# Loading expert weights 2 MB at a time, 16 KB to a partition, with two more buffers, in a mixture-of-experts encoder layer

## The chip, the cores and the metric

The kernel runs on one core of one Trainium2 chip. The metric is the device time of one execution in microseconds, the median of the timed runs. Sizes are counted as in the profile's list of loads: 1 MB here is 1024 KB.

## What is computed

One layer of a bidirectional encoder over 512 tokens of width 1024, in float32: three token mixers in parallel, a cross-attention into 256 memory tokens, and a mixture of 16 experts in which every expert picks 64 tokens. The change touches the experts alone. Cut to them, the reference is:

```python
def ec_moe(h, router_w, w_gu, w_down):          # h: (1, 512, 1024)
    cap = 2 * n // 16                           # 64 tokens for each of 16 experts
    aff = jax.nn.softmax(logits, axis=-1)
    gates, idx = lax.top_k(jnp.swapaxes(aff, 1, 2), cap)
    xs = jax.vmap(lambda hb, ib: hb[ib])(h, idx)
    def expert(args):
        xe, wgu, wd = args                      # wgu: (1024, 4096), wd: (2048, 1024)
        gu = jnp.einsum('bcd,df->bcf', xe, wgu)
        ga, up = jnp.split(gu, 2, axis=-1)
        return jnp.einsum('bcf,fd->bcd', jax.nn.silu(ga) * up, wd)
    ys = lax.map(expert, (jnp.swapaxes(xs, 0, 1), w_gu, w_down))
```

An expert's weights are 16 MB of `expert_w_gu` and 8 MB of `expert_w_down`; all 16 experts together are 384 MB, each byte read once.

## The kernel before, in words

**Stages.** The mixers and the cross-attention come first (up to about 377 us in the profile), then the experts one after another, then a final norm and the store. A scheduler of the language places the instructions of each engine in one fixed order when the kernel is built; waits between engines are on semaphores.

**Buffers for expert weights.** `chunks` numbers the weights in pieces of 1 MB, 24 to an expert: pieces 0 to 15 are of `expert_w_gu` (piece j holds 128 of the 1024 input rows, `j // 2`, and one half of the 4096 columns, `j % 2`), pieces 16 to 23 of `expert_w_down`. A buffer of 2048 words on each of 128 partitions, a *slot*, holds one piece. Slots are cut from regions of SBUF (`rc`, `r1`, `rq`, `r2a`, `rd`, `ra`, `rb`, `f0`, `rp`, `fb`) as the earlier stages let go of them: `open_slots` makes one and has it filled at once by `issue`, which takes the next number of `order` and starts the load on SP's queue. There are 22 slots, of which four (two `acc` in `f0`, one in `rp`, one in `fb`) are filled once; when the last matmul on a piece in one of the other 18 has been written down, `done` calls `issue` again for that slot. So 22 MB are loaded before the first expert begins.

**A load of `expert_w_gu`** (L868) moves 128 rows of 2048 floats, 8 KB contiguous for each partition. **A load of `expert_w_down`** (L876) views the matrix as `(k p) d -> p k d`: partition p gets row p of two blocks of 128 rows, two runs of 4 KB. The last expert's `expert_w_down` is cut by columns (`LAST`, 512, 256 and 256 wide), with runs of 2 KB and 1 KB, so that the final norm can begin early.

**The matmuls.** For each half of the columns and each input block, L1251 multiplies the 64 gathered tokens with 512 columns of the piece at a time, into the two 64-partition halves `ab` of a PSUM bank. The columns for `ab` are four runs of 128 words with 128 words between them:

```python
wv = w.f[:, b * 1024:(b + 1) * 1024].rearrange("p (i ab c) -> p i ab c", ab=2, c=128)
T.matmul(pg[2 * half + b][64 * ab:64 * ab + 64], xs.f[:, k, el * 64:(el + 1) * 64],
         wv[:, :, ab], start=(k == 0), stop=(k == KT - 1))
```

After SiLU and product (L1263, L1264), L1267 turns eight 128-wide blocks so that the inner features lie on partitions, and L1282 multiplies them with `expert_w_down`, one piece for two of its 16 blocks of 128 inner features. The scatter of expert e - 1 (L1208, L1209, L1218) and, every other expert, the gather of the next two (L1180) are placed among these. L1316 is the last expert's product with `expert_w_down`.

In the profile each of these float32 matmuls stands as two PE instructions (eight for one piece of 1 MB).

Of the kernel before, what the change touches and what calls it, by code (L numbers as in the profile page):

```python
# [98 lines left out]
def build(nc, tc, A, out, ne=NE, dbg=None):  # L99
# [82 lines left out]
    idn = ident.f  # L182
# [652 lines left out]

    slots = []
    gu = A["expert_w_gu"][0]
    wd = A["expert_w_down"][0]
    chunks = [(e, j) for e in range(ne) for j in range(24)]

    where = {}
    once = {}
    order = list(range(15)) + list(range(16, 22)) + [15] + list(range(22, len(chunks)))
    order = iter(order)


    LAST = (512, 256, 256)

    def down_part(e, j):

        if e < ne - 1:
            return 2 * (j - 16), 2, 0, D
        j, c = j - 16, 0
        for w in LAST:
            n = w // 128
            if j < n:
                return 16 // n * j, 16 // n, c, w
            j, c = j - n, c + w

    def issue(s):  # L860
        i = next(order, None)
        if i is None:
            return
        where[i] = s
        e, j = chunks[i]
        if j < 16:
            src = gu[e, (j // 2) * 128:(j // 2 + 1) * 128, (j % 2) * 2048:(j % 2 + 1) * 2048]
            SP.dma_start(s.f, src)  # L868
        else:
            v = wd[e].rearrange("(k p) d -> p k d", p=128)  # L870
            k, nk, c, nc_ = down_part(e, j)
            d, v = s.f.rearrange("p (k d) -> p k d", k=nk), v[:, k:k + nk, c:c + nc_]

            h = nk // 2 if i in (22, len(chunks) - 1) else nk
            for a in range(0, nk, h):
                SP.dma_start(d[:, a:a + h], v[:, a:a + h])  # L876

    def open_slots(arena, n, use=None):
        for _ in range(n):
            s = Buf(arena, [SLOT])  # L880
            if use:
                once.setdefault(use, []).append(s)
            issue(s)

    ss2, rs2, tm2, sc2 = (sm.f[:, 16 + 4 * i:20 + 4 * i] for i in range(4))
# [423 lines left out]
    for i, w in enumerate(LAST):  # L1309
        py = (SC if i % 2 else MM)()[:, :w]  # L1310
        for _ in range(w // 128):
            k, nk, _, _ = down_part(ne - 1, next(parts))
            wv = chunk().f.rearrange("p (k d) -> p k d", k=nk)
            for j in range(nk):
                ab, blk = (k + j) % 2, (k + j) // 2
                T.matmul(py[64 * ab:64 * ab + 64], hT.f[:, blk, 64 * ab:64 * ab + 64], wv[:, j],  # L1316
                         start=(blk == 0), stop=(blk == 7))
        split(py, flat(yh.f)[:, c0:c0 + w], flat(yl.f)[:, c0:c0 + w])
# [88 lines left out]
```

## Time and profile before

| | before |
|---|---|
| median of 3 runs | 1320.96 us (1319.33 to 1323.13) |
| the profiled execution | 1321.95 us |
| its span on the core | 1320.2 us |
| PE busy | 1227.5 us (93%) |
| DVE, ACT, POOL busy | 448.4, 273.7, 115.8 us |
| moved by DMA | 434.87 MB (of 10^6 bytes) |

The span is the time from the core's first instruction to its last in one profiled execution; the execution's own time is 1.75 us longer. "Busy" is the union of an engine's instructions. In the views, DMA is the mean busy share of the core's 16 DMA engines, GB/s what they moved, and PEclk the granted clock of TensorE as a share of full speed.

### The profile page before, as it was taken

The numbers are of one execution on the slowest core, as the hardware profiler recorded it, in microseconds if no ns is written. First come the engines' busy times: TensorE is split into PE (matmuls) and PEld (weight loads), VectorE is DVE, ScalarE is ACT, GpSimd is POOL, SyncE is SP. The second block draws the span as 40 slices with busy tenths as digits, with TensorE's granted clock in tenths as the row PEclk, the third lists the DMA queues.
The fourth block names the chain that finished last, engine by engine and source line by source line (L and its number), as shares of the span: only waits on it lengthen the run. The fifth ranks groups of instructions, "written<-read, shape, count | busy, mean of one in ns | idle before, by whom it ended". The sixth has DMA issues, their size and how long they took to land.

```text
span 1320.2 us, 15788 instructions
## 1 busy us (share of the span) xinstructions
PE 1227.5 (93%) x6257; PEld 625.9 (47%) x6257; DVE 448.4 (34%) x1035; ACT 273.7 (21%) x579; POOL 115.8 (9%) x157
## 2 busy tenths in 40 slices
PE   9899898999989999999999899889989998998885
PEld 9887587788843343343343243224323322432223
DVE  5998758626730212212312122121202121221313
ACT  6565644315401001010010101000000101010013
POOL 5433143103000000000000000000000000000012
PEclk9999999999999999999999999999999999999998
DMA  8221040317879999999999999999999999999995
GB/s 290 81 65 49 20 161 33 128 35 308 322 273 367 418 416 419 417 417 415 419 414 421 414 421 414 419 416 417 418 415 420 413 421 414 421 414 419 417 409 207
DMA packets 97338, 434.87 MB, mean 329 GB/s; under 512 B 7536, under 2 KB 25584, under 8 KB 64496
## 3 DMA queue, kind: packets, MB, share of 16 engines
q1 hardware_dynamic: 97264, 433.87, 82.2%
q8 instruction: 49, 0.80, 0.2%
q14 instruction: 25, 0.20, 0.0%
HBM read 431.74 MB, written 2.10 MB: 329 GB/s over the span
## 4 chain that ended last, share of the span: by engine, by line
PE 60%; DMA 25%; DVE 8%; ACT 3%; issue 1%; SPq 0%; POOL 0%; DVEq 0%; ACTq 0%; POOLq 0%
PE mm L1251 19%; PE sc L1282 9%; PE oo L1251 6%; PE tr L1180 5%; DMA r_f<-in_expert_w_down 5%; DMA rq_f<-in_expert_w_gu 5%; DMA rq_f<-in_expert_w_down 3%; DMA ra_f<-in_expert_w_down 3%; DMA rb_f<-in_expert_w_gu 3%; DMA r2a_f<-in_expert_w_gu 3%; PE mm L125 3%; PE mm L127 3%; PE mm L126 3%; PE tr L1208 2%; PE tr L1209 2%; DMA r_f<-in_expert_w_gu 2%
## 5 line engine op out<-in xcount | busy, mean ns | idle before, releaser
L1218 DVE SCALAR_TENSOR_TENSOR f_f<-tr,f_f 128x512 f32<-128x512 f32 x112 | 79.9, 746 | 91.5 <-PE tr L1209 91.5
L1251 PE MATMUL mm<-rq_f,rg_f 128*64 128x512 f32 x388 | 97.3, 604 | 6.8 <-DMA rq_f<-in_expert_w_gu 6.8
L133 DVE TENSOR_TENSOR rp_r<-sc,rp_r 128x512 fp32r<-128x512 f32 (+1 forms) x31 | 21.1, 682 | 215.7 <-ACT rp_r L132 215.7
L1251 PE MATMUL mm<-r_f,rg_f 128*64 128x512 f32 x324 | 80.3, 602 | 5.8 <-DMA r_f<-in_expert_w_gu 5.4
L1180 PEld LDWEIGHTS tr<-f_f 128*128 128x128 f32 x512 | 61.7, 191 | 45.5 <-issue 23.5
L1301 POOL TENSOR_SCALAR f_f<-f_f 128x128 f32<-128x128 f32 x8 | 3.3, 434 | 907.5 <-PE tr L1196 880.4
L1264 DVE TENSOR_TENSOR fb_f<-mm,fb_f 128x512 f32<-128x512 f32 x16 | 11.1, 692 | 205.3 <-PE mm L1251 199.4
L1180 PE MATMUL tr<-f_f 128*128 128x128 f32 x512 | 70.8, 284 | 7.5 <-ACT rg_f L1187 4.7
L1263 ACT ACTIVATE fb_f<-mm 128x512 f32<-128x512 f32 x32 | 19.0, 597 | 279.0 <-PE mm L1251 279.0
L1187 ACT ACTIVATE rg_f<-tr,f_f 128x128 f32<-128x128 f32 x32 | 11.8, 368 | 271.7 <-PE tr L1180 181.6
L1282 PE MATMUL sc<-rq_f,fb_f 128*64 128x512 f32 x280 | 64.6, 599 | 3.6 <-DMA rq_f<-in_expert_w_down 3.6
L1185 DVE TENSOR_SCALAR rg_f<-tr,f_f 128x128 f32<-128x128 f32 x32 | 11.2, 351 | 157.6 <-PE oo L1251 78.7
L1251 PE MATMUL mm<-rb_f,rg_f 128*64 128x512 f32 x240 | 59.6, 603 | 4.1 <-DMA rb_f<-in_expert_w_gu 4.1
L1282 PE MATMUL sc<-r_f,fb_f 128*64 128x512 f32 x240 | 57.3, 600 | 4.3 <-DMA r_f<-in_expert_w_down 4.3
L1208 PE MATMUL tr<-rp_r 128*128 128x512 f32 (+1 forms) x132 | 58.2, 444 | 3.3 <-ACT rp_r L132 1.4
L132 ACT CAST rp_r<-sc 128x512 fp32r<-128x512 f32 (+1 forms) x31 | 17.9, 579 | 199.6 <-PE sc L1282 199.6
L1209 PE MATMUL tr<-rp_r 128*128 128x512 f32 (+1 forms) x132 | 53.2, 407 | 1.8 <-DVE rp_r L133 1.1
L1208 PEld LDWEIGHTS tr<-rp_r 128*128 128x128 f32 x132 | 24.5, 187 | 55.8 <-DVE f_f L1218 31.5
L1251 PEld LDWEIGHTS mm<-rq_f,rg_f 128*64 128x64 f32 x388 | 24.3, 136 | 55.7 <-issue 34.6
L1251 PE MATMUL mm<-r2a_f,rg_f 128*64 128x512 f32 x192 | 46.5, 603 | 3.3 <-DMA r2a_f<-in_expert_w_gu 3.3
L127 PE MATMUL mm<-r_r,rb_r 128*128 128x256 f32 (+2 forms) x160 | 47.4, 300 | 0.0
L1251 PE MATMUL oo<-rq_f,rg_f 128*64 128x512 f32 x172 | 45.1, 593 | 0.0
(451 smaller groups left out, 2207.8 us busy)
## 6 DMA issues: line engine op xcount, KB each, us to landing
rq_f<-in_expert_w_gu SPq DMA_DIRECT2D x70, 1024.0 KB, 19.8
r_f<-in_expert_w_gu SPq DMA_DIRECT2D x54, 1024.0 KB, 19.8
rb_f<-in_expert_w_gu SPq DMA_DIRECT2D x45, 1024.0 KB, 19.8
rq_f<-in_expert_w_down SPq DMA_DIRECT2D x35, 1024.0 KB, 19.9
r2a_f<-in_expert_w_gu SPq DMA_DIRECT2D x32, 1024.0 KB, 19.8
r_f<-in_expert_w_down SPq DMA_DIRECT2D x30, 1024.0 KB, 20.0
ra_f<-in_expert_w_gu SPq DMA_DIRECT2D x26, 1024.0 KB, 19.9
rb_f<-in_expert_w_down SPq DMA_DIRECT2D x18, 1024.0 KB, 18.8
```

The lines of the kernel that those rows point to most:

```text
L125: T.matmul(o, lh, rh, start=start, stop=False)
L126: T.matmul(o, lh, rl, start=False, stop=False)
L127: T.matmul(o, ll, rh, start=False, stop=stop)
L132: C.copy(h.bitcast(F32R), src)
L133: (le or V).tensor_tensor(l.bitcast(F32R), src, h, op=ALU.subtract)
L1180: i = T.matmul(o, x.f[:, t, kt * 128:(kt + 1) * 128], flat(g.f[:, t]), start=(t == 0), stop=(t == NT - 1))
L1208: T.matmul(pp[:, i * w:(i + 1) * w], GT.r[:, ts_], flat(yh.r)[:, cs], start=True, stop=False)
L1209: T.matmul(pp[:, i * w:(i + 1) * w], GT.r[:, ts_], flat(yl.r)[:, cs], start=False, stop=True)
L1218: V.scalar_tensor_tensor(ao, p, g, ao, op0=ALU.mult, op1=ALU.add)
L1251: T.matmul(pg[2 * half + b][64 * ab:64 * ab + 64], xs.f[:, k, el * 64:(el + 1) * 64], wv[:, :, ab], start=(k == 0), stop=(k == KT - 1))
L1263: C.activation(hsl.f[:, b], pg[b], AF.Silu)
L1282: T.matmul(py[c][64 * ab:64 * ab + 64], hT.f[:, blk, 64 * ab:64 * ab + 64], wv[:, ab, c * 512:(c + 1) * 512], start=(blk == 0), stop=(blk ...
```

## The change

Seven things change together.

1. Slots are 4096 words now (2 MB), except one each in `rc`, `rq`, `rd` and `rb` and the four that are filled once, which keep 2048 words.
2. When a 2 MB slot takes an even piece and the one after it, both come in one load: for `expert_w_gu` 128 rows of 4096 floats, 16 KB contiguous to a partition.
3. The inner features are interleaved over the partitions: `expert_w_down` is viewed as `(c p r) d`, so that partition p holds rows 4p to 4p + 3 of a block of 512 rows. A 2 MB load then has 16 KB contiguous to a partition, a 1 MB load 8 KB. To match, column c of a 1024-wide block of `expert_w_gu` goes to half `ab = c % 2` (every other word is read by a matmul), and the transposes at L1267 take every other column of `hsl`.
4. A slot is refilled when all pieces in it are used (`s.left`).
5. A new region `ex` of 4096 words, from space that the build had kept for descriptors of software-made DMAs (`dynamic_dma_scratch_size=512`), holds one more 2 MB slot. It is opened right after the weave of `att_0`, in the first stage.
6. The first expert's 24 pieces are all loaded ahead, in a new `order`.
7. The last expert's column slices have the same run lengths as before; its 256-wide pieces are loaded in two halves each.

```diff
-WORDS = {"rp": 3072, "rg": 1024, "ra": 4096, "rb": 6144, "rc": 2048, "rd": 2048, "r2a": 4096, "r1": 8448, "rq": 10240, "fb": 2048}
-WORDS["f0"] = 53000 - sum(WORDS.values())
+WORDS = {"rp": 3072, "rg": 1024, "ra": 4096, "rb": 6144, "rc": 2048, "rd": 2048, "r2a": 4096, "r1": 8448, "rq": 10240, "fb": 2048, "ex": 4096}
+WORDS["f0"] = 57096 - sum(WORDS.values())
...
+    order = [0, 1, 2, 3, 4, 6, 7, 8, 9, 10, 11, 5, 12, 13, 14, 16, 18, 19, 22, 20, 21, 17, 23, 15]
+    order += range(24, len(chunks))
...
+    def load_chunk(i, d):
+
+        e, j = chunks[i]
+        n = d.shape[-1] // SLOT
+        if j < 16:
+            src = gu[e, (j // 2) * 128:(j // 2 + 1) * 128, (j % 2) * 2048:(j % 2 + n) * 2048]
+            dma = SP.dma_start(d, src)
+            if i < 2:
+                tc.keep_in_program_order(dma)
+            return
+        k, nk, c, w = down_part(e, j)
+        nk *= n
+        if nk < 3:
+            r = 2 * (k % 2)
+            v = wd[e].rearrange("(c p r) d -> c p r d", p=128, r=4)[k // 2, :, r:r + 2 * nk, c:c + w]
+            SP.dma_start(d.rearrange("p (r d) -> p r d", d=w), v)
+        else:
+            v = wd[e].rearrange("(c p r) d -> p c r d", p=128, r=4)[:, k // 2:(k + nk) // 2, :, c:c + w]
+            d = d.rearrange("p (c r d) -> p c r d", r=4, d=w)
+            for a in range(nk // 2):
+                SP.dma_start(d[:, a], v[:, a])
+
+    def issue(s):
+        n = s.n // SLOT
+        ids, order[:n] = order[:n], []
+        for a, i in enumerate(ids):
+            where[i] = s, s.f[:, a * SLOT:(a + 1) * SLOT]
+        s.left = len(ids)
+        if n == 2 and ids and ids[0] % 2 == 0 and ids[1] == ids[0] + 1 and ids[0] < len(chunks) - 8:
+            load_chunk(ids[0], s.f)
+        else:
+            for i in ids:
+                load_chunk(i, where[i][1])
...
     run(fill)
+    open_slots(Arena(sp, "ex"), 1)
     for t in range(NT):
         turn(t, QT)
...
-    def done(s):
-        if id(s) not in kept:
+    def done(w):
+        s = w[0]
+        s.left -= 1
+        if not s.left and id(s) not in kept:
             issue(s)
...
-                    wv = w.f[:, b * 1024:(b + 1) * 1024].rearrange("p (i ab c) -> p i ab c", ab=2, c=128)
+                    wv = w[1][:, b * 1024:(b + 1) * 1024].rearrange("p (c ab) -> p ab c", ab=2)
...
-                T.transpose(p[:, i * 128:(i + 1) * 128], hsl.f[:, b, i * 128:(i + 1) * 128], idn)
+                T.transpose(p[:, i * 128:(i + 1) * 128], hsl.f[:, b, i // 2 * 256 + i % 2:(i // 2 + 1) * 256:2], idn)
...
-    nc = _bacc.Bacc("TRN2", target_bir_lowering=False, num_devices=1)
+    nc = _bacc.Bacc("TRN2", target_bir_lowering=False, num_devices=1, dynamic_dma_scratch_size=512)
```

What the built program issues differs most on SP, which starts the loads. Of the kernel before, the last 20 of one steady expert's 24 loads (names are the region that is written, `r1` without its number, and the tensor that is read; x4 is four loads in a row):

```order
L868 DMA rd_f<-in_expert_w_gu 128x2048
L868 DMA ra_f<-in_expert_w_gu 128x2048 x2
L868 DMA rb_f<-in_expert_w_gu 128x2048 x3
L868 DMA r_f<-in_expert_w_gu 128x2048 x2
L868 DMA rc_f<-in_expert_w_gu 128x2048
L868 DMA r_f<-in_expert_w_gu 128x2048 x2
L868 DMA rq_f<-in_expert_w_gu 128x2048
L876 DMA rq_f<-in_expert_w_down 128x2x1024 x4
L876 DMA r2a_f<-in_expert_w_down 128x2x1024 x2
L876 DMA rd_f<-in_expert_w_down 128x2x1024
L876 DMA ra_f<-in_expert_w_down 128x2x1024
```

The same stretch of SP in the changed program, one steady expert without its last load, an `rb` of 2 MB:

```order
L500 DMA ra_f<-in_expert_w_gu 128x4096
L500 DMA rb_f<-in_expert_w_gu 128x4096
L500 DMA ex_f<-in_expert_w_gu 128x4096
L500 DMA r_f<-in_expert_w_gu 128x4096
L500 DMA rc_f<-in_expert_w_gu 128x2048
L500 DMA rq_f<-in_expert_w_gu 128x2048
L500 DMA r_f<-in_expert_w_gu 128x4096
L500 DMA rq_f<-in_expert_w_gu 128x4096 x2
L509 DMA r2a_f<-in_expert_w_down 128x4096
L509 DMA rd_f<-in_expert_w_down 128x2048
L509 DMA rb_f<-in_expert_w_down 128x2048
L509 DMA ra_f<-in_expert_w_down 128x4096
```

Two loads in three are twice as large, the others stay at 1 MB, and the order of the pieces is the same. Counted over the whole program, behind the first 24 pieces come 96 loads of 2 MB and 48 of 1 MB of `expert_w_gu`, and 45 of 2 MB and 22 of 1 MB of `expert_w_down` before the last expert's slices.

In the first stage SP's rows around the new early load, in the changed program (L224 loads the mixers' weights, of which the first four shown are two sets and the next two the third set, `pl`; L807 loads the memory tokens):

```order
L224 DMA rq_f<-in_w_in 128x4x264 x3
L224 DMA rq_f<-in_w_in 128x4x256 x4
L500 DMA ex_f<-in_expert_w_gu 128x4096
L224 DMA rq_f<-in_w_in 128x4x256 x2
L224 DMA rq_f<-in_ca_wkv 128x4x256 x2
L807 DMA rq_f<-in_memT 128x4x256 x2
```

Before, the six loads of 128x4x256 stand there without a break; on the other engines the rows ahead of the first expert are unchanged.

## Rows read from the trace of the kernel before

**Rows 1.** From the profile's page: busy time of PE, and the span in 40 equal slices (33 us each) with the granted clock, the DMA engines' busy share in tenths, and GB/s.

```profile
PE 1227.5 (93%) x6257; PEld 625.9 (47%) x6257; DVE 448.4 (34%) x1035; ACT 273.7 (21%) x579; POOL 115.8 (9%) x157
...
PE   9899898999989999999999899889989998998885
...
PEclk9999999999999999999999999999999999999998
DMA  8221040317879999999999999999999999999995
GB/s 290 81 65 49 20 161 33 128 35 308 322 273 367 418 416 419 417 417 415 419 414 421 414 421 414 419 416 417 418 415 420 413 421 414 421 414 419 417 409 207
```

**Rows 2.** The chain of work that ended last, in order of time, over the last expert: start, length, what.

```profile
1221.04 20.37 DMA ra_f<-in_expert_w_down
...
1241.47 19.82 DMA r_f<-in_expert_w_gu
...
1261.36 19.83 DMA r2a_f<-in_expert_w_gu
...
1281.23 1.08 PE mm L1251 x4
```

**Rows 3.** PE's instructions in order of time while it multiplies the last expert's `expert_w_gu`: the first and the last of eight groups that begin with the landing of a load (in brackets the idle time before, and what ended it).

```profile
1263.82 1.94 PE L1251 MATMUL mm<-r_f,rg_f 128*64 128x512 f32 x8 [0.42 <-DMA r_f<-in_expert_w_gu]
1266.31 1.08 PE L1251 MATMUL mm<-rq_f,rg_f 128*64 128x512 f32 x4 [0.55 <-DMA rq_f<-in_expert_w_gu]
...
1281.23 1.08 PE L1251 MATMUL mm<-r2a_f,rg_f 128*64 128x512 f32 x4 [0.55 <-DMA r2a_f<-in_expert_w_gu]
```

**Rows 4.** The same for the `expert_w_down` of the expert before it: the five groups that begin with a landing.

```profile
1231.24 1.94 PE L1282 MATMUL sc<-rq_f,fb_f 128*64 128x512 f32 x8 [0.61 <-DMA rq_f<-in_expert_w_down]
1233.90 1.94 PE L1282 MATMUL sc<-r2a_f,fb_f 128*64 128x512 f32 x8 [0.71 <-DMA r2a_f<-in_expert_w_down]
...
1241.45 1.94 PE L1282 MATMUL sc<-ra_f,fb_f 128*64 128x512 f32 x8 [0.60 <-DMA ra_f<-in_expert_w_down]
```

**Rows 5.** DMA packets in two stretches: 1242 to 1281 us, mostly `expert_w_gu`, and 1221 to 1241 us, mostly `expert_w_down` (here MB of 10^6 bytes).

```profile
DMA packets 2702, 16.27 MB, mean 417 GB/s; under 512 B 250, under 2 KB 250, under 8 KB 873
```

```profile
DMA packets 1966, 8.23 MB, mean 412 GB/s; under 512 B 127, under 2 KB 127, under 8 KB 1797
```

**Rows 6.** Stretches of time: length, then busy us (and count) of PE, of its weight loads, of DVE, ACT and POOL, PEclk, the DMA share and GB/s. The early load's place, and the first expert's beginning.

```profile
64.00:82.00 18.00, 16.54 (x106) 15.30 (x107) 17.19 (x56) 14.77 (x40) 5.22 (x10) 0.91 0.20 58
...
360.00:380.00 20.00, 15.26 (x77) 9.17 (x75) 13.82 (x73) 1.75 (x6) 1.20 (x2) 0.83 0.60 241
380.00:430.00 50.00, 50.00 (x249) 19.82 (x250) 3.29 (x7) 4.55 (x8) 0.00 (x0) 1.00 0.92 359
430.00:480.00 50.00, 49.06 (x244) 20.94 (x242) 11.06 (x23) 4.42 (x9) 0.00 (x0) 1.00 1.02 418
```

**Rows 7.** The same columns for the experts' stage in two parts.

```profile
377.00:760.00 383.00, 375.05 (x1777) 145.55 (x1779) 70.28 (x132) 35.40 (x66) 0.00 (x0) 1.00 1.00 407
760.00:1283.00 523.00, 477.81 (x2161) 170.31 (x2159) 95.43 (x162) 40.67 (x75) 1.89 (x4) 1.00 1.02 417
```

**Rows 8.** The same two parts for the instructions of L1251 alone (busy us of its matmuls and of its weight loads).

```profile
377.00:760.00 383.00, 203.83 (x898) 60.41 (x900) 1.00 1.00 407
760.00:1283.00 523.00, 271.35 (x1152) 72.40 (x1150) 1.00 1.02 417
```

**Rows 9.** SP's queue in order of time: loads of the mixers' weights in the first stage, and the last load ahead of the first expert with the first refills.

```profile
62.74 2.56 SPq L224 DMA_DIRECT2D rq_f<-in_w_in  x2
...
81.59 0.37 SPq L224 DMA_DIRECT2D rq_f<-in_w_in  x1
```

```profile
362.57 0.34 SPq L868 DMA_DIRECT2D fb_f<-in_expert_w_gu  x1
378.20 4.19 SPq L876 DMA_DIRECT2D r_f<-in_expert_w_down  x3
```

**Rows 10.** From the groups by line: L1251, which reads four runs of 128 words, and L1282, which reads one run of 512, both with 512 columns: count, busy us, mean ns of one, idle time before and what ended it.

```profile
L1251 PE MATMUL mm<-rq_f,rg_f 128*64 128x512 f32 x388 | 97.3, 604 | 6.8 <-DMA rq_f<-in_expert_w_gu 6.8
...
L1282 PE MATMUL sc<-rq_f,fb_f 128*64 128x512 f32 x280 | 64.6, 599 | 3.6 <-DMA rq_f<-in_expert_w_down 3.6
```

**Rows 11.** L1267's weight loads (the turned blocks of `hsl`): shortest, median and longest in ns, first and last start.

```profile
L1267 PEld LDWEIGHTS tr<-f_f,fb_f x128: 137/140/144, 419.4 to 1284.3; 128*128 128x128 f32 x128
```

**Rows 12.** PE at the end: the last product with `expert_w_down`.

```profile
1303.92 1.95 PE L1316 MATMUL mm<-r_f,fb_f 128*64 128x256 f32 x16
```

More of the change, by code (lines that the diff above doesn't have):

```diff
@@ L466, in attention, with down_part, open_slots @@
             yield from finish()
+    gu = A["expert_w_gu"][0]
+    wd = A["expert_w_down"][0]
+    chunks = [(e, j) for e in range(ne) for j in range(24)]
+    where = {}
+    once = {}
+    order = [0, 1, 2, 3, 4, 6, 7, 8, 9, 10, 11, 5, 12, 13, 14, 16, 18, 19, 22, 20, 21, 17, 23, 15]
+    order += range(24, len(chunks))
+    LAST = (512, 256, 256)
+    def down_part(e, j):
+        if e < ne - 1:
+            return j - 16, 1, 0, D
+        j, c = j - 16, 0
+        for w in LAST:
+            n = w // 128
+            if j < n:
+                return 8 // n * j, 8 // n, c, w
+            j, c = j - n, c + w
+    def load_chunk(i, d):
[29 more added lines that the diff above has]
+                load_chunk(i, where[i][1])
+    def open_slots(arena, n, use=None, words=2 * SLOT):
+        for _ in range(n):
+            s = Buf(arena, [SLOT if use else words])
+            if use:
+                once.setdefault(use, []).append(s)
+            issue(s)
     qe.free()
@@ L833, in build @@
     run(out_proj(0))
[L836 to L883, printed above, removed]
     ss2, rs2, tm2, sc2 = (sm.f[:, 16 + 4 * i:20 + 4 * i] for i in range(4))
@@ L1084, in build @@
         SP.dma_start(wo_raw.f[:, k:k + 2], wo_src[:, k:k + 2])
-    open_slots(r1, 2)
-    open_slots(Arena(sp, "rc"), 1)
+    open_slots(r1, 1)
+    open_slots(Arena(sp, "rc"), 1, words=SLOT)
     def ca_w():
@@ L1107, in build @@
         b.free()
-    open_slots(r1, 2)
+    open_slots(r1, 1)
     junk = Buf(r1, [256])
     jk3 = junk.f.bitcast(BF16)
-    open_slots(Arena(sp, "rq"), 5)
-    open_slots(Arena(sp, "r2a"), 2)
+    rq = Arena(sp, "rq")
+    open_slots(rq, 2)
+    open_slots(rq, 1, words=SLOT)
+    open_slots(Arena(sp, "r2a"), 1)
     fill = ca_out(0)
@@ L1118, in build @@
     open_slots(f0, 1, "acc")
-    open_slots(Arena(sp, "rd"), 1)
-    open_slots(Arena(sp, "ra"), 2)
+    open_slots(Arena(sp, "rd"), 1, words=SLOT)
+    open_slots(Arena(sp, "ra"), 1)
     open_slots(f0, 1, "acc")
@@ L1126, in build @@
         b.free()
-    open_slots(Arena(sp, "rb"), 3)
+    rb = Arena(sp, "rb")
+    open_slots(rb, 1)
+    open_slots(rb, 1, words=SLOT)
     open_slots(Arena(sp, "rp"), 1, "yh")
@@ L1248, in build @@
                 for b in range(2):
-                    wv = w.f[:, b * 1024:(b + 1) * 1024].rearrange("p (i ab c) -> p i ab c", ab=2, c=128)
+                    wv = w[1][:, b * 1024:(b + 1) * 1024].rearrange("p (c ab) -> p ab c", ab=2)
                     for ab in range(2):
                         T.matmul(pg[2 * half + b][64 * ab:64 * ab + 64], xs.f[:, k, el * 64:(el + 1) * 64],
-                                 wv[:, :, ab], start=(k == 0), stop=(k == KT - 1))
+                                 wv[:, ab], start=(k == 0), stop=(k == KT - 1))
                 done(w)
@@ L1278, in build @@
             w = chunk()
-            wv = w.f.rearrange("p (ab d) -> p ab d", ab=2)
+            wv = w[1].rearrange("p (ab d) -> p ab d", ab=2)
             for c in range(2):
@@ L1312, in build @@
             k, nk, _, _ = down_part(ne - 1, next(parts))
[L1313 to L1317, printed above, removed]
+            wv = chunk()[1].rearrange("p (k ab d) -> p k ab d", k=nk, ab=2)
+            for blk in range(k, k + nk):
+                for ab in range(2):
+                    T.matmul(py[64 * ab:64 * ab + 64], hT.f[:, blk, 64 * ab:64 * ab + 64], wv[:, blk - k, ab],
+                             start=(blk == 0), stop=(blk == 7))
         split(py, flat(yh.f)[:, c0:c0 + w], flat(yl.f)[:, c0:c0 + w])
```

## The prediction

> **What bounds the kernel now.** I read the sliced page first. From the fourteenth slice on (429 us) the DMA engines are busy in every slice and move 413 to 421 GB/s until the last two, while PE is busy 93% of the span at a granted clock of 0.9 to 1.0 of full speed [rows 1]. Two engines near full say nothing about which one sets the end, so the chain comes next. Over the last expert it runs from load to load, each about 20 us from issue to landing, until the first matmuls on the last load of `expert_w_gu` at 1281.23 us [rows 2]. PE's order in time shows the same from the other side: it stands idle 0.4 to 0.7 us before each group, until a load lands [rows 3, 4]. So the last expert goes at the pace of the loads. Earlier it does not: from 377 to 760 us PE is busy 375 of 383 us, and only from 760 to 1283 us does it have slack, 523 - 477.8 = 45.2 us [rows 7]. PE eats a backlog first and waits for loads afterwards; since the DMA engines are full from 430 us on (share 1.02, [rows 6]), the end is the sum of the loads.
>
> The pace of a load is then what matters. For `expert_w_gu`, eight groups begin between 1263.82 and 1281.23 us, seven loads apart: 17.41 / 7 = 2.487 us for 1 MB [rows 3]. For `expert_w_down`, 1231.24 to 1241.45 us over four loads: 10.21 / 4 = 2.553 us [rows 4]. Both are 1 MB in one load; what differs is the run, 8 KB against 4 KB. In the stretch with `expert_w_down` 1797 of 1966 packets are under 8 KB and carry 8.23 MB, in the other 873 of 2702 with 16.27 MB [rows 5]: a run is a packet, 128 to a load of the one, 256 to a load of the other. The 128 more cost 2.553 - 2.487 = 0.066 us, half a nanosecond for each.
>
> **Term 1, longer runs.** A run of 16 KB makes 64 packets of a MB. If the cost of a packet goes on as between 4 KB and 8 KB, 1 MB takes 2.487 - 0.033 = 2.454 us. No row shows a 16 KB run of a load. Bounds: nothing gained over 8 KB (the engine cuts it in two), or all that packets cost gone (0.066 us below 8 KB). I take the straight line, as the nearest pair of rows gives it. The first 24 pieces are loaded ahead and are not on the path. Behind them:
> - `expert_w_gu`, 96 loads of 2 MB: 192 x 0.033 = 6.3 us; its 48 loads of 1 MB keep 8 KB runs, 0.
> - `expert_w_down`, 45 loads of 2 MB: 90 x (2.553 - 2.454) = 8.9 us; 22 of 1 MB go from 4 KB to 8 KB, 22 x 0.066 = 1.5 us.
>
> Together 16.7 us. The last expert's slices keep their runs: 0.
>
> **Term 2, two more MB ahead.** Before the first expert the loads run dry: 362.57 us is the last issue, 378.20 us the next [rows 9], and the engines move 241 GB/s from 360 to 380 us and 359 from 380 to 430 us, against 418 [rows 6]. They wait for slots there. Two MB more are worth at most 2 x 2.49 = 5.0 us. But a 2 MB slot is refilled only after its second piece, about one load time (2.5 us) later than now; at worst that takes all of it. I take 2 us of 0 to 5. The early load itself costs nothing: from 64 to 82 us the engines are busy a fifth of the time and move 58 GB/s [rows 6], and between SP's issues up to 65.3 us and the next one at 81.59 us [rows 9] there are 16 us, of which it needs 5.
>
> **What I cost at nothing.** Two pieces now land together every 4.9 us instead of one every 2.49. PE needs 1.94 us for a piece [rows 3], so 3.9 of 4.9 us: it still waits for the next load. At the end one more piece is left after the last `expert_w_gu` load (+1.9 us), but the last expert's `expert_w_down` keeps landing, and its last product starts only at 1303.92 us [rows 12], 20 us later; that is the cover. L1267 reads every other column: a weight load takes 140 ns [rows 11]; doubled, it adds 8 x 0.14 = 1.1 us to an expert, against 45.2 us of slack over nearly nine experts, and once at the end behind the same cover. SP issues fewer loads, and no engine's rows ahead of the first expert move.
>
> The edit that may cost is the matmul that reads every other word at L1251. Before it reads four runs with gaps, at 604 ns, and L1282 reads one run, at 599 [rows 10]; a step of two is not in the trace. Bounds: nothing, or each L1251 matmul at half rate, which adds its whole busy time again, 203.8 + 271.4 = 475 us [rows 8]. I take nothing, as the nearest row says that a gapped read costs 5 ns of 600, and keep the rest as a rival. [...]
>
> **The sum.** 16.7 + 2 = 18.7 us. The profiled execution took 1321.95 us (a span of 1320.2 and 1.75 around it), so 1303.3; it lies 0.99 us above the median of 1320.96, so I say 1302.3 us. Within 0.3% (4 us) a run of this kernel can't be told from no change.
>
> **Rivals.**
> - *16 KB runs are cut, or no faster than 8 KB.* For it: no row has one. Against: 4 to 8 KB did gain. Then only `expert_w_down` gains, (90 + 22) x 0.066 = 7.4 us, with term 2 9.4: 1311.6 us. Chance 0.15.
> - *The stepped read slows PE: slower than before.* Place: L1251. PE is busy 852.9 of the 906 us from 377 to 1283 [rows 7], so it can take 53 us more before the end passes the old one: 11% on L1251's 475 us. From (53 - 19) / 475 = 7% on it begins to eat the gain. At 25% it adds 119 us: 1321 + 119 - 53 = 1387; at half rate 1321 + 475 - 53 = 1743 us. For it: nothing in the trace reads so; against: gaps cost nothing so far. Chance 0.13.
> - *Coarse slots starve the loads.* The refill waits of 2.5 us recur until the backlog is long (380 to 430 us), and without the 16 KB gain: three such waits, 7.5 us, eat the 7.4 us of the rival above: 1321 us, no change. Against: PE frees pieces faster than loads come once DMA is full. Chance 0.07.
> - *A fixed time for each load.* If the engines paused between two loads, 141 merged pairs would save 141 pauses. Against: their share is 1.02 from 760 us on [rows 7]; a pause has no room in it. If 0.3 us were hidden in each: 42 us less, 1279 us; PE's slack of 53 us would still cover it. Chance 0.03. [...]
>
> **How the numbers follow.** My forecast has 0.62; the rivals 0.15, 0.13, 0.07 and 0.03. Its bounds: 16 KB with all packet cost gone, 192 x 0.066 + 90 x 0.132 + 1.5 = 26.1, and 5 us of term 2: 31 us, 1290; at the other end only 7.4 us of gain and nothing of term 2, 1313.6. I give 1291 to 1315, which leaves out the slow rival, no change and the fixed time, and a little of the forecast's own edge. Faster: 0.62 + 0.15 + 0.03, less 0.01: 0.79. Within 0.3%: 0.07. Slower: 0.13, and 0.01 for a mishap of the starving kind: 0.14.
>
> **What would show it.** In the changed profile, PE's groups that begin with a landing should lie 4.9 us apart for 2 MB loads of either tensor. 4.97 us would say that a 16 KB run is no better than two of 8 KB. GB/s in the late slices should be about 427, against 413 to 421. L1251 should keep about 600 ns; eight matmuls taking more than 2.1 us, or a PE without idle time late in the span, is the slow rival. From 360 to 430 us the DMA share tells of the slots: below 0.6 and 0.92 is starving. The packet count should fall by near half in the late stretches. I would be wrong above all if PE had no slack left for what it reads with a step.

## The result and the profile after

The changed kernel takes 1305.24 us (median of 4 runs, 1304.71 to 1308.04), the kernel before 1321.28 us beside it: a ratio of 0.9883, 95% interval 0.9863 to 0.9903. The profiled execution took 1304.99 us, 16.96 us less than that of before; 18.7 us less were forecast. All runs of this document are compared with the kernel before as it ran beside them, 1321 to 1325 us.

From the page of the changed kernel, busy time, the share and rate of the DMA engines in 40 slices, and the packets:

```profile
PE 1233.3 (95%) x6257; PEld 635.2 (49%) x6257; DVE 451.7 (35%) x1035; ACT 272.8 (21%) x579; POOL 117.4 (9%) x157
...
DMA  8231051306868999999999999999999999999995
GB/s 291 73 139 51 17 166 34 129 33 257 329 242 366 394 426 428 425 425 426 425 427 427 424 429 425 424 428 426 426 426 427 424 426 428 425 427 426 426 405 189
DMA packets 60552, 434.85 MB, mean 334 GB/s; under 512 B 5184, under 2 KB 23232, under 8 KB 31424
```

Where the loads had moved 413 to 421 GB/s [rows 1], they move 424 to 429 now. PE in order of time over the last loads of `expert_w_gu`, to be read against [rows 3] (L1276 is the old L1251, L1341 the old L1316):

```profile
1252.92 2.92 PE L1276 MATMUL mm<-r_f,rg_f 128*64 128x512 f32 x12 [1.58 <-DMA r_f<-in_expert_w_gu]
1255.68 1.07 PE L1276 MATMUL oo<-r_f,rg_f 128*64 128x512 f32 x4
1257.82 2.92 PE L1276 MATMUL mm<-rq_f,rg_f 128*64 128x512 f32 x12 [1.08 <-DMA rq_f<-in_expert_w_gu]
1260.58 1.07 PE L1276 MATMUL oo<-rq_f,rg_f 128*64 128x512 f32 x4
1262.78 2.92 PE L1276 MATMUL mm<-rq_f,rg_f 128*64 128x512 f32 x12 [1.14 <-DMA rq_f<-in_expert_w_gu]
1265.54 1.06 PE L1276 MATMUL oo<-rq_f,rg_f 128*64 128x512 f32 x4
1266.57 0.74 PE L1292 MATMUL tr<-f_f,fb_f 128*128 128x128 f32 x4
```

Groups of 16 matmul instructions, two pieces, begin 4.90 and 4.96 us apart, each when a load has landed. Two such distances can't be told from twice 2.487 us; over the trace from 500 us on, a 2 MB load lands 4.90 us behind the load before it in the median: 2.45 us for 1 MB. Behind the last landing stand 16 instructions, 3.8 us, where there were eight. The chain that ended last still runs from load to load, but not without a break:

```profile
1184.13 34.34 DMA r2a_f<-in_expert_w_down
1218.61 7.10 PE sc L1307 x32
...
1228.41 34.33 DMA rq_f<-in_expert_w_gu
1262.78 2.92 PE mm L1276 x12
```

These loads land 34 us after their issue (20 in [rows 2]): at 2.45 us for 1 MB that makes some 14 MB in the queue, by my estimate, where 20 us at 2.487 make eight, and between two loads of the chain PE works 7 us on `expert_w_down`. Busy time, clock, DMA share and GB/s by stage, as [rows 6, 7]:

```profile
64.00:82.00 18.00, 16.20 (x105) 15.11 (x106) 17.20 (x55) 14.44 (x38) 5.21 (x10) 0.91 0.48 176
360.00:380.00 20.00, 15.28 (x77) 9.40 (x76) 13.87 (x73) 1.75 (x6) 1.20 (x2) 0.83 0.55 233
380.00:430.00 50.00, 50.00 (x241) 19.55 (x242) 3.29 (x7) 4.54 (x8) 0.00 (x0) 1.00 0.82 327
430.00:480.00 50.00, 49.04 (x234) 21.15 (x231) 10.70 (x22) 3.86 (x8) 0.00 (x0) 1.00 1.01 426
377.00:760.00 383.00, 375.46 (x1732) 146.12 (x1734) 69.27 (x129) 34.05 (x64) 0.00 (x0) 1.00 0.98 410
760.00:1266.00 506.00, 486.41 (x2206) 181.99 (x2202) 96.39 (x164) 41.45 (x77) 2.40 (x4) 1.00 1.01 426
```

The loads go at full rate (426 GB/s) from 430 us on; PE's slack from 760 us to the last gate/up matmul has shrunk from 45.2 to 19.6 us: the stretch is 17 us shorter, and PE is busy 8.6 us longer in it. The same stages for L1276 alone, against [rows 8]:

```profile
377.00:760.00 383.00, 212.88 (x896) 60.69 (x896) 1.00 0.98 410
760.00:1266.00 506.00, 270.65 (x1152) 76.33 (x1152) 1.00 1.01 426
```

212.88 us over 896 instructions is 237.6 ns of PE for each; before it was 203.83 over 898, 227.0 ns: 4.7% more. Behind 760 us these rows don't show the step, 234.9 ns against 235.5, but there PE stopped for a load every eight instructions before [rows 3], and every 16 now; gapread, below, has the same loads and the old read.

**One table for all kernels.** The stage before the experts holds the same work in all of them, yet in the profiled executions the first gate/up matmul starts anywhere from 374.5 to 385.6 us, with a granted clock of 0.93 to 0.97 from 200 us to it. So I count from that matmul. "80 MB" is when the packets that have ended, summed over the trace, reach 80 MB (good to some 0.3 us); the next column is the time of the 310 MB behind. The columns from "last landed" on count from the first matmul too. All in us.

| kernel | first matmul | to 80 MB | next 310 MB | last `expert_w_gu` landed | last gate/up matmul ended | end of span |
|---|---|---|---|---|---|---|
| before | 377.1 | 84.9 | 779.6 | 904.1 | 906.1 | 943.2 |
| before_ex | 376.3 | 81.8 | 779.5 | 901.3 | 903.3 | 940.5 |
| layout | 380.7 | 86.2 | 772.0 | 898.3 | 900.4 | 937.6 |
| single | 374.5 | 83.6 | 772.1 | 895.9 | 897.9 | 935.3 |
| swap | 376.7 | 84.2 | 771.9 | 896.1 | 900.0 | 938.0 |
| changed | 377.2 | 83.7 | 762.7 | 885.5 | 889.4 | 926.1 |
| gapread | 379.0 | 81.9 | 762.7 | 884.0 | 887.7 | 924.5 |
| tail | 378.9 | 83.6 | 762.8 | 885.8 | 888.2 | 925.8 |
| piece24 | 385.6 | 84.6 | 762.8 | 886.6 | 890.4 | 928.3 |
| both | 375.5 | 84.6 | 762.8 | 886.9 | 889.7 | 927.1 |
| kept | 376.3 | 81.2 | 764.0 | 886.5 | 890.4 | 927.1 |
| best | 376.3 | 79.9 | 763.8 | 882.8 | 886.7 | 923.4 |

Of the 16.96 us, 1.2 were won up to 80 MB, 16.9 in the next 310 and 0.5 behind them (18.6 at the last landing); 1.9 were lost on the piece more that PE has left there, 0.4 came back in the tail, and the first matmul itself stands 0.1 later.

### The profile page after: what moved, and what is told of

Read it like the earlier page. It is cut to its first block, busy times and chain, and to the rows that moved or that the text cites. A ratio compares the mean times of both kernels' runs of the same rounds, so it can differ in the third digit from the quotient of the medians.

```text
span 1303.3 us, 15488 instructions
## 1 busy us (share of the span) xinstructions
PE 1233.3 (95%) x6257; PEld 635.2 (49%) x6257; DVE 451.7 (35%) x1035; ACT 272.8 (21%) x579; POOL 117.4 (9%) x157
## 2 busy tenths in 40 slices
DMA packets 60552, 434.85 MB, mean 334 GB/s; under 512 B 5184, under 2 KB 23232, under 8 KB 31424
## 4 chain that ended last, share of the span: by engine, by line
PE 66%; DMA 18%; DVE 10%; ACT 3%; issue 1%; SPq 0%; POOL 0%; DVEq 0%; ACTq 0%; POOLq 0%
PE mm L1276 21%; PE sc L1307 13%; PE oo L1276 7%; DMA rb_f<-in_expert_w_gu 5%; PE tr L1203 5%; PE mm L125 3%; PE mm L127 3%; PE mm L126 3%; DMA r2a_f<-in_expert_w_gu 3%; DMA r2a_f<-in_expert_w_down 3%; DMA rq_f<-in_expert_w_gu 3%; DMA rq_f<-in_expert_w_down 2%; PE tr L1231 2%; PE tr L1232 1%; DVE f_f L1241 1%
## 5 line engine op out<-in xcount | busy, mean ns | idle before, releaser
L1276 PE MATMUL mm<-rq_f,rg_f 128*64 128x512 f32 x364 | 91.7, 618 | 2.2 <-DMA rq_f<-in_expert_w_gu 2.2
L1326 POOL TENSOR_SCALAR f_f<-f_f 128x128 f32<-128x128 f32 x8 | 3.8, 493 | 890.4 <-PE tr L1219 864.3
L1276 PE MATMUL mm<-r_f,rg_f 128*64 128x512 f32 x312 | 76.8, 617 | 1.6 <-DMA r_f<-in_expert_w_gu 1.6
L1307 PE MATMUL sc<-rq_f,fb_f 128*64 128x512 f32 x240 | 54.2, 595 | 0.2 <-DMA rq_f<-in_expert_w_down 0.2
L1276 PEld LDWEIGHTS mm<-rq_f,rg_f 128*64 128x64 f32 x364 | 24.3, 134 | 51.0 <-issue 45.5
L1276 PE MATMUL mm<-rb_f,rg_f 128*64 128x512 f32 x192 | 48.9, 619 | 0.0
L126 PE MATMUL mm<-r_r,ra_r 128*128 128x256 f32 (+2 forms) x152 | 43.9, 292 | 0.6 <-POOL r_r L133 0.6
L125 PE MATMUL mm<-r_r,ra_r 128*128 128x256 f32 (+2 forms) x152 | 43.2, 293 | 1.1 <-ACT r_r L132 0.7
L1307 PE MATMUL sc<-r_f,fb_f 128*64 128x512 f32 x192 | 43.3, 593 | 0.0
```

Of the source, the lines that this page charges most:

```text
L125: T.matmul(o, lh, rh, start=start, stop=False)
L126: T.matmul(o, lh, rl, start=False, stop=False)
L1307: T.matmul(py[c][64 * ab:64 * ab + 64], hT.f[:, blk, 64 * ab:64 * ab + 64], wv[:, ab, c * 512:(c + 1) * 512], start=(blk == 0), stop=(blk ...
```

## The experiments

**layout: the interleaved layout alone.**

```diff
-    order = [0, 1, 2, 3, 4, 6, 7, 8, 9, 10, 11, 5, 12, 13, 14, 16, 18, 19, 22, 20, 21, 17, 23, 15]
-    order += range(24, len(chunks))
+    order = list(range(15)) + list(range(16, 22)) + [15] + list(range(22, len(chunks)))
...
-            s = Buf(arena, [SLOT if use else words])
+            for _ in range(1 if use else words // SLOT):
+                s = Buf(arena, [SLOT])
...
-    open_slots(Arena(sp, "ex"), 1)
```

> The interleaved layout alone: 1 MB slots and loads as in the kernel before, 22 of them, no region ex, no load of 16 KB runs; expert_w_down has 8 KB runs instead of 4 KB, and the gate/up matmul reads every other word. Theory (the length of the runs sets the pace of the loads, the stepped read is paid by PE out of its slack): loads of expert_w_down land every 2.49 us instead of 2.55, those of expert_w_gu every 2.487 as before; 112 loads behind the lead, 112 x 0.066 = 7.4 us less than the kernel before, 1314 us (1312 to 1316). PE's busy time grows by some 24 us (4.7% on 475 us of gate/up matmuls) without moving the end. Rival (the stepped read lies on the path): 1321 to 1335 us. Rival (only the number of loads counts, not their runs): the same time as before, 1321 us.

Measured: ratio 0.9957 (0.9941 to 0.9974), a median of 1317.46 us beside 1323.53 for the kernel before. PE in order of time on `expert_w_down` of the last expert but one, against [rows 4]:

```profile
1231.53 1.94 PE L1306 MATMUL sc<-r2a_f,fb_f 128*64 128x512 f32 x8 [0.73 <-DMA r2a_f<-in_expert_w_down]
1233.92 1.94 PE L1306 MATMUL sc<-r2a_f,fb_f 128*64 128x512 f32 x8 [0.46 <-DMA r2a_f<-in_expert_w_down]
1236.41 1.94 PE L1306 MATMUL sc<-rd_f,fb_f 128*64 128x512 f32 x8 [0.55 <-DMA rd_f<-in_expert_w_down]
1238.89 1.94 PE L1306 MATMUL sc<-ra_f,fb_f 128*64 128x512 f32 x8 [0.55 <-DMA ra_f<-in_expert_w_down]
```

Loads of `expert_w_down` land 2.39, 2.49 and 2.48 us apart now; over 310 MB 7.6 us are saved, as the theory had it, about 103 loads by 0.074 us, and no load is saved: the rival by which only their number counts is wrong for this step. But the start is 1.3 us later (86.2 to 80 MB, not 84.9), and only 5.7 us reach the last matmul; the forecast of 7.4 us was too much. The later start is the stepped read, as gapread shows below: the rival that has it on the path is wrong in size, right in that the read isn't free. PE as a whole is busy 1246.7 us, 19.2 more than before, where 24 were expected.

**single, swap and halfpart: run length or number of loads.** In single, the pairs are loaded piece by piece:

```diff
-        if n == 2 and ids and ids[0] % 2 == 0 and ids[1] == ids[0] + 1 and ids[0] < len(chunks) - 8:
+        if n == 3 and ids and ids[0] % 2 == 0 and ids[1] == ids[0] + 1 and ids[0] < len(chunks) - 8:
```

> The changed kernel, but each piece of a 2 MB slot has its own load of 1 MB with 8 KB runs; both are still started together when the slot is free. Theory (run length): every load lands 2.485 us after the one before, against 4.90 for 2 MB in the changed kernel; 141 pairs x (4.97 - 4.90) = 10 us more in the stream, 1.9 us less behind its end because the last piece of gate/up is alone again: 1313 us (1311 to 1315). Rival (a fixed time for each load, 141 loads more): the same 10 us here, told apart by the run with half the partitions. Rival (16 KB is no better than 8 KB): 1303 us.

In halfpart, a pair comes in two loads of 64 partitions, 16 KB to each:

```diff
-    def load_chunk(i, d):
+    def load_chunk(i, d, p0=0, p1=128):
...
-            dma = SP.dma_start(d, src)
+            dma = SP.dma_start(d[p0:p1], src[p0:p1])
...
-            load_chunk(ids[0], s.f)
+            for p in (0, 64):
+                load_chunk(ids[0], s.f, p, p + 64)
```

> The changed kernel, but each 2 MB pair comes in two loads of 64 partitions each: the number of loads of the kernel before the change, 1 MB each, with runs of 16 KB. Theory (run length): a pair still lands every 4.90 us, 1305 us (1303 to 1307). Rival (a fixed time for each load): a pair takes 4.97 us as in two loads of 8 KB runs, 141 x 0.07 = 10 us more, 1315 us. [...]

In swap, one load brings the pair, but its two pieces change places in the slot, so that no run is longer than 8 KB:

```diff
+            if n == 2:
+                d, src = (v.rearrange("p (a c) -> p a c", a=2) for v in (d[:], src))
+                d = d[:, ::-1]
             dma = SP.dma_start(d, src)
...
```

> The changed kernel, but a 2 MB load writes the two pieces of its pair in swapped order into the slot, so that a run is 8 KB; the number of loads, their size, the slots and the matmuls are those of the changed kernel. Theory (run length): a pair lands every 4.97 us as from two loads of 8 KB runs, 310 MB of the stream take 772 us as in the run with single loads instead of 763; 1305 + 9 = 1314 us. Rival (a fixed time for each load, or for each start): pairs land every 4.90 us, 763 us for 310 MB, 1305 us.

Measured: single 1316.33 us (ratio 0.9941, 0.9926 to 0.9957), swap 1316.39 us (0.9948, 0.9929 to 0.9967), halfpart 2108.18 us (2064.44 to 2187.23 in 6 runs). PE in single over the last loads:

```profile
1262.86 2.02 PE L1276 MATMUL mm<-rq_f,rg_f 128*64 128x512 f32 x8 [0.47 <-DMA rq_f<-in_expert_w_gu]
1265.34 1.12 PE L1276 MATMUL mm<-rq_f,rg_f 128*64 128x512 f32 x4 [0.45 <-DMA rq_f<-in_expert_w_gu]
1266.29 1.07 PE L1276 MATMUL oo<-rq_f,rg_f 128*64 128x512 f32 x4
1267.83 2.02 PE L1276 MATMUL mm<-rq_f,rg_f 128*64 128x512 f32 x8 [0.48 <-DMA rq_f<-in_expert_w_gu]
```

1262.86 to 1267.83 is 4.97 us for two MB. Single (1311 to 1315 expected) and swap (1314) came out a little above their forecasts, as did the kernel before beside them (1323.53 and 1322.55). The page of swap, DMA rate by slices and packets:

```profile
GB/s 290 79 132 49 18 165 33 128 33 289 330 244 335 423 420 421 421 421 421 422 421 421 421 420 421 421 421 421 422 421 421 421 420 421 421 421 421 421 399 176
DMA packets 79624, 434.85 MB, mean 331 GB/s; under 512 B 5184, under 2 KB 23232, under 8 KB 31424
```

421 GB/s, and 771.9 us for 310 MB against 772.1 in single: 141 loads fewer change nothing, while the run alone, 8 KB or 16 KB with the same loads, makes 9.2 us (a 2 MB load lands 4.97 us behind the one before it in the median). Swap reads the same 16 KB rows from memory as the changed kernel; only the pieces that they are moved in are shorter (79624 packets where that has 60552). The rival of a fixed time for each load is wrong.

halfpart can't tell, because its loads go at half the rate. Busy time by engine, clock, DMA share and GB/s of its middle:

```profile
1000.00:1800.00 800.00, 504.87 (x1696) 174.33 (x1692) 72.13 (x131) 32.70 (x61) 0.00 (x0) 0.80 1.01 214
```

The DMA engines are busy all the time (share 1.01) and move 214 GB/s, half of the 426 of the changed kernel. Why two loads of 64 partitions go slower isn't shown.

**before_ex: two more MB ahead of the kernel before, in 1 MB slots.**

```diff
+    open_slots(Arena(sp, "ex"), 2)
     for t in range(NT):
         turn(t, QT)
...
```

(Besides, the region `ex` and `dynamic_dma_scratch_size=512` as in the change, the code of the slots further up, and pieces 22 and 23 ahead too.)

> The kernel before with the region ex as two slots of 1 MB, opened where the changed kernel opens its one slot of 2 MB: two more MB ahead at the old granularity, nothing else changed. Theory (the loads wait for slots between 372 and 436 us, and each MB more ahead saves one load there): 4 to 5 us less than the kernel before, 1316 to 1317 us. Rival (the first refills are set by PE's pace, so that more ahead only lets the loads rest longer): 1321 us, within 1.

Measured: 1320.58 us, ratio 0.9979 (0.9966 to 0.9991): 2.8 us less. 80 MB are moved 3.1 us earlier after the first matmul, and these 3 us stay to the end (903.3 instead of 906.1). The theory's 4 to 5 us were too many: by the sums of packets 5.2 us are won when 56 MB are moved, and 3.2 are left at 70 MB. Added to layout (2.8 + 5.7 = 8.5 us) it nearly makes single (906.1 - 897.9 = 8.2): slots of 2 MB and the order that goes with them, which single has beyond the two, cost at most some tenths of a us at the end, and 83.6 - (84.9 - 3.1 + 1.3) = 0.5 us at 80 MB.

**gapread: the changed kernel with the old read.**

```diff
-                    wv = w[1][:, b * 1024:(b + 1) * 1024].rearrange("p (c ab) -> p ab c", ab=2)
+                    wv = w[1][:, b * 1024:(b + 1) * 1024].rearrange("p (i ab c) -> p ab i c", ab=2, c=128)
```

> The changed kernel, but the gate/up matmul reads its columns as before, in four runs of 128 words with gaps, which pairs the inner features with the wrong rows of expert_w_down; loads, slots and all else as in the changed kernel. Theory (PE pays 4.7% for the step and has the slack): the gate/up matmuls go back from 238 to 227 ns of PE time each, PE is busy 22 to 25 us less, and the end moves by 0 to 2 us (first refills come 1 to 2 us earlier): 1303 to 1305 us. Rival (the step is on the path, PE is the bound): 1293 us or less. Rival (the step costs nothing and the longer busy time has another cause, such as landings into the same memory): busy time as in the changed kernel.

Measured: 1305.24 us, ratio 0.9850 (0.9831 to 0.9869). The kernel leaves out the matching of inner features and rows of `expert_w_down`; its work is the same. L1276 alone:

```profile
377.00:760.00 383.00, 203.37 (x896) 61.72 (x896) 1.00 0.97 410
760.00:1266.00 506.00, 261.83 (x1150) 77.74 (x1152) 1.00 1.01 426
```

203.37 / 896 = 227.0 ns: the whole price is the step, 9.5 us in the stage in which PE has next to no slack, and 8.8 us behind 760 us (227.7 ns an instruction, not 234.9). 1.8 of them reach 80 MB (81.9 instead of 83.7) and 1.6 the end (924.5 instead of 926.1). The rest comes out of PE's waits for loads behind 760 us, as the theory said. PE as a whole is busy 1217.9 us, 15.4 less than in the changed kernel; 22 to 25 were expected.

**reads: what a read pattern costs.** Eight lines, one for each input block:

```diff
-                    wv = w[1][:, b * 1024:(b + 1) * 1024].rearrange("p (c ab) -> p ab c", ab=2)
...
+                        elif k == 2:
+                            T.matmul(oo, xk, u.rearrange("p (i ab c) -> p ab i c", ab=2, c=4)[:, ab], **se)
```

> The changed kernel, but the gate/up matmul reads its 512 columns in another pattern for each of the eight input blocks k, from eight lines: k = 0 every other word, 1 runs of two words, 2 of four, 3 of 16, 4 of 128, each with gaps as long, 5 one run of 512, 6 every fourth word, 7 two words of eight; the outputs are therefore other sums. Only the busy time of each line is asked, per instruction. [...] Rival (the price is one of the gaps, whatever their place): all of k = 0 to 4 at 238 ns, which the run with the gapped read already speaks against.

The outputs are other sums, so only the lines are read, not the time (1345.01 us, one run). One group of PE instructions of each line (count, busy us, mean ns; L1281 is k = 0, L1283 k = 1 and so on to L1295, k = 7):

```profile
L1293 PE MATMUL mm<-rq_f,rg_f 128*64 128x512 f32 x48 | 22.7, 1077 | 0.0
L1283 PE MATMUL mm<-r_f,rg_f 128*64 128x512 f32 x84 | 21.6, 619 | 0.0
L1287 PE MATMUL mm<-r_f,rg_f 128*64 128x512 f32 x84 | 19.5, 596 | 0.0
L1295 PE MATMUL mm<-r_f,rg_f 128*64 128x512 f32 x72 | 17.7, 626 | 0.0
L1291 PE MATMUL mm<-r_f,rg_f 128*64 128x512 f32 x72 | 16.6, 596 | 0.0
L1289 PE MATMUL mm<-rq_f,rg_f 128*64 128x512 f32 x60 | 14.3, 596 | 0.0
L1285 PE MATMUL mm<-rq_f,rg_f 128*64 128x512 f32 x52 | 13.5, 602 | 0.0
L1281 PE MATMUL mm<-rq_f,rg_f 128*64 128x512 f32 x48 | 12.4, 622 | 0.0
```

Runs of 4, 16, 128 and 512 words: 596 to 602 ns. Every other word 622, runs of two 619, two words of eight 626: what counts is that two words of a group of four are used, not how far it is to the next group. Every fourth word, one of four: 1077, near half rate. So the rival is wrong: the runs of 4, 16 and 128 words have gaps as long as themselves, and cost at most 6 ns more than the one of 512.

**tail: the last pair in two loads.**

```diff
-        if n == 2 and ids and ids[0] % 2 == 0 and ids[1] == ids[0] + 1 and ids[0] < len(chunks) - 8:
+        if n == 2 and ids and ids[0] % 2 == 0 and ids[1] == ids[0] + 1 and ids[0] < len(chunks) - 10:
```

> The changed kernel, but the last pair of expert_w_gu comes in two loads of 1 MB. Theory (behind the last landing PE still works on all that landed with it, and nothing covers this): the last piece lands 0.07 us later, but 8 matmuls less follow it, 1.8 us less than the changed kernel, 1303.4 us. Rival (the last product waits for its own weights anyway, as the prediction has it): no difference, 1305.2 us.

Measured: 1308.67 us, ratio 0.9874 (0.9851 to 0.9897), which can't be told from the changed kernel. By the table, the last gate/up matmul ends 2.4 us after the last landing instead of 3.9, and 1.2 us earlier after the first; but the tail behind it is 37.6 us instead of 36.7, so that 0.3 us are left. PE there:

```profile
1266.05 1.06 PE L1276 MATMUL oo<-rq_f,rg_f 128*64 128x512 f32 x4
...
1269.65 1.94 PE L1341 MATMUL mm<-r2a_f,fb_f 128*64 128x512 f32 x8
1271.52 1.16 PE L1327 MATMUL tr<-f_f 128*128 128x128 f32 x8
1272.61 1.94 PE L1341 MATMUL mm<-r2a_f,fb_f 128*64 128x512 f32 x8
```

No wait for a load stands in these rows or between them: the rival (the product waits for its own weights) is wrong in its reason, though the time can't be told from the one it gave. The scheduler wove transposes and product in another order, so what a split pair is worth by itself stays open; the 1.4 us between landing and last matmul are shown.

**piece24 and both: refilling piece by piece during the first expert.**

```diff
         s.left -= 1
+        done.n += 1
+        if done.n <= 24 and id(s) not in kept:
+            i = order.pop(0)
+            where[i] = s, w[1]
+            load_chunk(i, w[1])
+            s.left += 1
+            return
...
```

> The changed kernel, but while the first expert's 24 pieces are being used each piece of a slot is refilled by itself as soon as it is free, by a load of 1 MB; later refills are of whole slots again. Theory (the second piece of a slot holds back the first refills): the loads start again at 379 us instead of 382, 70 MB are moved some 4 us earlier, 16 pieces go in 8 KB runs (0.6 us lost): 3 to 4 us less than the changed kernel, 1301.5 us (1300.5 to 1303). Rival (the refills go at PE's pace in any case): 1305 us.

> The two edits of tail and piece24 together. Theory: they lie in different places and add up, 1.8 + 3.5 = 5.3 us less than the changed kernel, 1300 us (1299 to 1302). If PE has become the bound in the middle, the earlier loads give less: 1303 us.

Measured: piece24 1306.46 us (0.9871, 0.9847 to 0.9896), both 1307.65 us (0.9875, 0.9854 to 0.9896): no gain. The first refill in the changed kernel, whose first gate/up matmul is at 377.20 us, and SP's issues in piece24, where it is at 385.62 us:

```profile
382.30 0.33 SPq L500 DMA_DIRECT2D ex_f<-in_expert_w_gu  x1
```

```profile
387.68 3.37 SPq L500 DMA_DIRECT2D ex_f<-in_expert_w_gu  x2
...
417.96 2.13 SPq L500 DMA_DIRECT2D r2a_f<-in_expert_w_gu  x2
433.66 0.33 SPq L509 DMA_DIRECT2D ex_f<-in_expert_w_down  x1
```

The refills start 2.1 us after the first matmul instead of 5.1, but between 420 and 433.66 us no slot comes free, and the loads rest longer there. 80 MB take 84.6 us, 1 more than before the edit. The theory of the coarse slots is wrong; the rival, PE's pace, is right.

**kept and best.** In kept the slots that are never refilled hold pieces that are used late; best also leaves the first expert, all of whose pieces are loaded ahead, the old layout and with it the old read:

```diff
-    order = [0, 1, 2, 3, 4, 6, 7, 8, 9, 10, 11, 5, 12, 13, 14, 16, 18, 19, 22, 20, 21, 17, 23, 15]
+    order = [0, 1, 2, 3, 4, 6, 7, 8, 9, 10, 11, 5, 12, 13, 17, 14, 18, 19, 22, 20, 21, 16, 23, 15]
...
+                    if e:
+                        wv = wv.rearrange("p (c ab) -> p ab c", ab=2)
+                    else:
+                        wv = wv.rearrange("p (i ab c) -> p ab i c", ab=2, c=128)
...
```

> The changed kernel, but the two slots acc, which are filled once, hold pieces 17 and 22 instead of 14 and 22, so that piece 14 lies in rd, which is refilled 38 us after the first expert's first matmul instead of 53. Theory (in the first 60 us the loads wait for the slots that PE lets go of; they run dry between 44 and 47 us after the first matmul): one more load lies in this gap, 70 MB are moved 2.4 us earlier after the first matmul (56.6 us instead of 59.05), and the last gate/up matmul ends 2.4 us earlier after the first one (887.0 us instead of 889.4); 1303 us. Rival (the slots that come free later are the limit, the load only waits elsewhere): 889.4 us and 1305 us.

> The same as kept, and the first expert alone keeps the layout of the kernel before (four runs of 128 words at the gate/up matmul, two 4 KB runs of expert_w_down, transposes of whole blocks), since all its pieces are loaded ahead. Theory (the stepped read costs something only where PE sets the pace, in the first expert): 16 pieces x 8 x 11 ns = 1.4 us less than kept, 55.2 us to 70 MB and 885.6 us from the first to the last gate/up matmul; 1301.5 us. Rival (the second expert's reads count as well, or the loads are not PE's to set): 0.5 us or less.

Measured: kept 1305.46 us (0.9868, 0.9850 to 0.9885), best 1301.79 us (0.9840, 0.9820 to 0.9860; 1298.76 to 1304.11 in 4 runs). In kept the 2.5 us are there at 80 MB, and about 1 us is left at 100 MB. Two stretches, 100 to 120 and 120 to 130 us after its first matmul (columns as above):

```profile
476.30:496.30 20.00, 20.00 (x102) 8.51 (x100) 1.30 (x3) 1.54 (x3) 0.00 (x0) 1.00 1.01 423
496.30:506.30 10.00, 10.00 (x48) 3.16 (x44) 0.00 (x0) 0.55 (x1) 0.00 (x0) 1.00 0.96 378
```

PE is busy in all of both, and the loads run dry a second time: in the second expert too slots come free no faster, which is the rival. Later in this execution four loads land 6.4 us after the one before them instead of 4.9 (in the changed kernel two, 6.0 and 6.1), and the last one is then 1 us later than in the changed kernel; why isn't settled. best, in which PE itself is faster in the first expert, keeps more of its gain: 3.8 us less to 80 MB, 2.7 us less to the last matmul and to the end. How much of the 3.7 us to kept at the last matmul is the read isn't shown: 1.3 are there at 80 MB, as expected. It is the fastest kernel here, though its interval (up to 0.9860) only just doesn't meet that of the changed kernel (from 0.9863), and meets that of kept.

## Why the prediction was right, and where not

**What bounds the kernel: right.** The end moved with the loads: 18.6 us at the last landing, 17.0 at the end.

**Term 1, 16.7 us: right, a little small.** The loads gave 16.9 us over the 310 MB and 0.5 behind them. The line through 4 KB and 8 KB goes on to 16 KB. 4 to 8 KB gave 7.6 us in layout (0.074 us a load, 0.066 assumed); 8 to 16 KB gave 772.1 - 762.7 = 9.4 us over 310 MB, of which 282 in 360 parts come in 2 MB loads, 243 MB: 0.039 us a MB where 0.033 was assumed. Both are 0.6 ns for a packet of a load, not 0.5. The sign named for it, 4.9 us from one 2 MB load to the next, came (4.90 in the median, 4.97 in swap), and the packets fell from 97338 to 60552. The rival by which 16 KB is no better than 8 KB fell with it.

**Term 2, 2 us: 1.2, and for another reason.** Two MB ahead are worth 3.1 us by themselves (before_ex), not 5. The prediction let coarse slots eat 3 of its 5; they took 0.5. The stepped read took 1.3 (layout) to 1.8 (gapread). That 2 came out near 1.2 is in part luck.

**The stepped read at nothing: the step that failed in its reasoning.** The rival's bound, 7% before it eats into the gain, was PE's slack summed over 906 us. But [rows 7] showed that the slack lies behind 760 us; in the first 60 us behind the first matmul PE has none (it is busy 50.00 of 50 us from 380 us on, [rows 6]), slots come free at its pace, and loads wait for slots. There 4.7% on 128 instructions of the first expert's 16 pieces is 128 x 10.6 ns = 1.4 us, and that is what was lost. Over the whole, 4.7% lay below the bound, so it cost no more.

**The cover of the last piece: wrong.** That the last product starts only 20 us later [rows 12] was no cover. PE's only waits of over 0.15 us between the last gate/up matmul and it, in the kernel before:

```profile
1284.04 0.66 PE L1267 MATMUL tr<-f_f,fb_f 128*128 128x128 f32 x4 [0.20 <-DVE fb_f L1264]
...
1294.67 0.73 PE L1208 MATMUL tr<-rp_r 128*128 128x512 f32 x2 [0.69 <-ACT rp_r L132]
```

It waits for no load there, so all of it moves with that matmul. The 1.9 us named in the same sentence were on the path: 3.9 us from the last landing to the last matmul, 2.0 before. Here lies the miss between 18.7 and 17.0, for 18.6 us had been won at the last landing.

**Early load, L1267, SP at nothing: right.** The first gate/up matmul stands at 377.20 us, before at 377.08. The weight loads that read every other column (L1292, the old L1267) do cost half as much again, 209 ns in the median for 140 [rows 11], less than the doubling that was allowed for. From the changed kernel:

```profile
L1292 PEld LDWEIGHTS tr<-f_f,fb_f x128: 194/209/219, 421.1 to 1267.8; 128*128 128x128 f32 x128
```

Four transposes take 0.74 us and 0.66 before, which makes 0.2 us within the last expert.

**The sign for starving misled.** The DMA share did fall from 360 to 430 us, to 0.55 and 0.82, below the 0.6 and 0.92 that were to mean starving. But 2 MB of what had been moved there now landed earlier, from 64 us on; the time at which 80 MB were moved tells it rightly, 1.2 us earlier.

## To carry to other kernels

Where queued loads fill the DMA engines, lengthen the run per partition: here, from 4 to 8 to 16 KB, each packet saved was worth the same, about 0.6 ns, and the number of loads nothing. Compare slack and cost stage by stage, not by sums: a price that PE pays "out of its slack" is paid in full wherever PE sets the pace (the stepped read took 1.3 to 1.8 us here), and more buffers help there only as far as PE lets go of them (of 2.5 us that kept won up to 80 MB, about 1 was left at 100 MB). What lands last is followed by all the work that waits for it (3.9 us here, with one piece more, instead of 2.0), so count that work onto the end unless a wait stands behind it.

## What was not expected of the hardware

- The matmul's moving operand: 596 to 602 ns with at least four words in a row, 619 to 626 with two words of each four used, 1077 with one (run reads).
- A weight load of 128x128 that reads every other column: 209 ns in the median, 140 without the step (changed kernel and before).
- Two loads of 64 partitions, 16 KB to each, go at 214 GB/s with the DMA engines busy all the time (share 1.01), where one of 128 partitions goes at 426 (run halfpart and changed kernel).
